# Attention ahead of RWKV, retention behind it, with banks reserved and new costs in a list scheduler

## The chip, the cores and the metric

The kernel runs on one core of one Trainium2 chip. The metric is the device time of one execution in microseconds (us). The kernel before takes 1000.04 us, the median of three executions (999.21 to 1001.67).

Engines go by their short names: PE is TensorE, DVE VectorE, ACT ScalarE, POOL GpSimd, and SP the queue that issues the DMAs.

## The reference, cut to what matters

Two layers over one sequence of 256 tokens, model width 1024. Each layer projects the normed input once, cuts the result into three branches and the gates, and mixes the branches:

```python
def hybrid_layer(x, ...):
    h = _rms(x) * norm1_g
    proj = h @ w_in                       # 1024 -> 768 + 1792 + 2048 + 3072 columns
    aq, ak, av, rw, rq, rk, rv, rg, gates = _split(proj, IN_SIZES)
    ...
    o_a = sliding_window_attention(aq, ak, av, attn_sinks) @ w_attn_o
    o_b = rwkv7_time_mix(rw, ...) @ w_rwkv_o      # a recurrence over tokens, then a group norm
    o_c = retention(rq, rk, rv, rg) @ w_ret_o     # chunks of 128, then a norm and a gate
    g = jax.nn.sigmoid(gates).reshape(B, T, N_BRANCH, D)
    mixed = g[:, :, 0] * o_a + g[:, :, 1] * o_b + g[:, :, 2] * o_c
    x = x + mixed @ w_out
    h2 = _rms(x) * norm2_g
    return x + (jax.nn.silu(h2 @ w_ffn_gate) * (h2 @ w_ffn_up)) @ w_ffn_down   # width 2816
```

The end of RWKV, to which one part of the change belongs, is `y = (y * lnx_g + lnx_b + bonus) * g` with `y` normed by head, `bonus` a row sum times `v`, and `g` a small product of its own.

## The kernel before, in words

**Weights.** All weights are fp32 and are read once, in 292 units of 512 KB. A unit comes by DMA into a tile `raw`, ACT casts it to `wh`, DVE takes `wl = raw - wh` (`wunit`), and PE then runs three products for every tile of output: `wh` with the input's high part, `wl` with the high part, `wh` with the input's low part (`mm3`). There are three tiles each of `raw`, `wh` and `wl`, so the `wl` of a unit can be written only when PE has done with the unit three places ahead of it. These products are called bulk here; each unit holds 12 of them with 512 columns (24 with 256 columns in RWKV's projection `pf`).

**Order.** Nothing is issued as it is written. A recording layer (`class Program`) keeps every operation with its reads and writes, and a list scheduler (`schedule`, `forward`) then puts them into one order per engine: it goes by a cost for each operation (`cost`), latencies between engines (`LAT_*`), and a priority that is mostly the longest path to the end (`bl`). Two things are fixed ahead of it: bulk products stand on PE exactly in the order in which they are recorded, and an engine works its list in order, so a row that waits holds up all rows behind it. PSUM has four banks for bulk results and four (`pss`) for everything small.

**One layer as it is recorded.** Projection `rq` with its rotary embedding; RWKV's projection `pf` in seven blocks; the rest of RWKV (`rwkv_rest`); attention's projections `aq`, `akv` and attention; projections `rk`, `rv`, `rg` and retention; then the gates' projections `gt` and the products `po` with the three output weights, in the order attention, retention, RWKV; `w_out` (`px`); the FFN (`pfg`, `pfu`, `pd`). "Recorded" settles the order of bulk; the small operations of a branch drift to where their inputs and the scheduler's priorities let them.

**What the steps below touch.** In RWKV, X, GA and GR are built from the projections; then DVE inverts 32 by 32 triangles by a chain of 31 pairs `prod`, `Tt` (`Tt` grows by one column a pair), and transposes the result twice into `M` and `Tn`; PE's `pz` reads `Tn`; a recurrence of four steps follows (`pr`, `pu`, `py`, `pd`). The end of RWKV for each half t of the tokens: reduce, POOL's power `ggr`, five products and sums on `ysb` (with `lnx`, `bv` and the product `pgt`), PE transposes `pto`, and a split into `obh` and `obl`, which the last bulk `po` reads. Retention for each half t: `pst`, a mask into `sT`, `po` (PE, from `rv_sb`, `sT` and for t = 1 `Rz`), a square on ACT (`rsq`), a reduce (`rvr`), POOL's power (`rrr`), two products (`o` on DVE, with `rrr` and with `rg_sb`), transposes `ptc`, and a split into `och` and `ocl`, which the bulk `po` of retention reads. Two different things carry the name `po`: bulk ones read `wh` or `wl`, small ones read `sT` or `Rz`.

All operations come from one place in the recording layer, so every row of the profile has the line L421 (L432 in the changed kernel), and rows are told apart by their tiles.

Of the kernel before, what the change touches and what calls it, by code (L numbers as in the profile page):

```python
# [27 lines left out]
LAT_SAME, LAT_X, LAT_IN, LAT_SIDE, LAT_OUT, LAT_DMA, LAT_ISSUE = 130, 150, 250, 400, 200, 930, 1290  # L28
# [79 lines left out]
class Program:  # L108
# [9 lines left out]
    def __init__(self, nc):  # L118
        self.nc, self.ops, self.acc, self.tiles, self.tags, self.bulk = nc, [], {}, {}, {}, False
        self.stream, self.split, self.urgent, self.unit, self.after = 0, False, False, 0, None  # L120
        self.bundle = None
# [35 lines left out]
    def cost(self, eng, method, args, kw, out, ins):  # L157
# [3 lines left out]
        if eng == "PE":  # L161
            if method == "transpose":
                return 109
            if kw["lhsT"].dtype == F32R:
                return 3 + n / 2.4
            c = max(4 + 4 * n / 2.4, 60)
            return c if out.ap[0][1] > 64 else (0.67 if out.ap[0][1] > 32 else 0.36) * c
        src = any(_psum(a) for a in ins)
        if eng == "DVE":
            if method == "reciprocal":  # L170
                return 69 + 6.3 * n
            if method == "tensor_reduce":
                n = 1
                for _, c in list(ins[0].ap)[1:]:
                    n *= c
            if method in ("tensor_copy", "tensor_scalar", "memset") and not src:
                return 69 + n / 1.92
            return 69 + n / 0.96
        if eng == "ACT":
            c = (51 if src else 94) + n / 1.2  # L180
            if _is_ap(kw.get("scale", 1.0)) or _is_ap(kw.get("bias", 0.0)):
                c += 25 if kw["func"] == AF.Copy and not src else 93
# [16 lines left out]
    def add(self, eng, method, fn, args, kw):  # L199
# [15 lines left out]
        touched = []  # L215
# [21 lines left out]
        if merged is not None:  # L237
            assert merged["eng"] == eng
            merged["calls"].append((fn, args, kw))
            merged["touch"].update(touched)  # L240
            merged["cost"] += cost
# [3 lines left out]
        self.ops.append(dict(eng=eng, calls=[(fn, args, kw)], preds=preds, touch=set(touched),  # L245
# [18 lines left out]
    def schedule(self):  # L264
# [15 lines left out]
        for i in range(n - 1, -1, -1):  # L280
            bl[i] = ops[i]["cost"] + max((bl[j] + l for j, l in succ[i]), default=0.0)
        return self.forward(succ, need, bl)

    def forward(self, succ, need, bl):
# [13 lines left out]
        parked = {}  # L298
# [21 lines left out]
        def blocked(i):  # L320
# [6 lines left out]
            for (k, q), ts_ in new.items():  # L327
# [6 lines left out]
                if len(free[k]) < taken[k]:  # L334
                    return k
# [93 lines left out]
def hybrid_kernel(ctx: ExitStack, tc: tile.TileContext, A: dict, cst_d: bass.AP, out: bass.AP, layers=L):  # L429
# [33 lines left out]
    def bc(ap, shape):  # L463
        return ap.to_broadcast(shape)
# [194 lines left out]
    for l in range(layers):  # L659
# [17 lines left out]

        def rope(ps, t):
# [13 lines left out]
        def rope_T(ps, dstT, keep=None):  # L692
            for t in range(2):
                t1, t2 = rope(ps, t)
                if keep is not None and t == 0:
                    qr = keep
                else:
                    qr = ST([128, 512], "qr")
                tt(qr, t1, t2, ADD)
                pt = PS([128, 512], "ptr")  # L700
                transposes(pt, qr)
                S.copy(dstT[:, :, t * 128:(t + 1) * 128], pt.rearrange("p (k t) -> p k t", k=4))

        rec.stream = 2
        ps = proj_tok(2560, 512, "rq")
        rqT = MT([128, 4, T], "rqT")
        rope_T(ps, rqT)
# [88 lines left out]
        def rwkv_rest():  # L796
# [45 lines left out]

            GA = RT([128, 4, 4, 64], "GA")
# [17 lines left out]

            BKT = [RT([128, 2, 4, 128], "BKT") for _ in range(2)]
            for i in range(2):
                for src in (na, EN):
                    pt = PS([128, 2, 2, 128], "ptb")
                    for j in range(2):
                        for d in range(2):
                            P.transpose(pt[:, j, d, :], src[:, 2 * i + j, d * 128:(d + 1) * 128], ident)
                    for par in range(2):
                        o_ = HR[par] if src is na else HR[1 - par]  # L870
                        cs = slice(64 * par, 64 * par + 64)
                        for ci in range(2):
                            S.copy(BKT[i].rearrange("p j (d c) v -> p j d c v", c=2)[o_, :, :, ci, cs], pt[HR[ci], :, :, cs])

# [52 lines left out]
            rk = RT([128, 4, T], "rk")  # L927
            for p in range(4):
                stt(rk[:, p, :], zr[:, p, :], vcol("rk", p), k2[:, p, :], MUL, MUL)
            pbs = head_sums(rk, "pbs")  # L930
            bsum = TL(sm_p, [128, 2, 8], F32, tag="bsum", name="bsum")
            S.copy(bsum.rearrange("p t (a b) -> p t a b", b=2), pbs)


            ysb = [RT([128, 8, 64], "ysb") for _ in range(2)]
            Sn = None
            for c in range(4):
# [4 lines left out]
                for p in range(4):  # L942
                    for par in range(2):
                        mm(pr[HR[par], p, :], X[p][:, par, c, 0:64], sv[:, p, par, :])
# [7 lines left out]
                for p in range(4):  # L952
                    for par in range(2):
                        mm(pu[HR[par], p, :], M[HR[par], p, c, :], RS[HR[par], p, :])
                S.copy(ysb[t][rr], py[rr])
                S.copy(sv[HR[0], :, 0, :], pu[HR[0]])
                S.copy(sv[HR[1], :, 1, :], pu[HR[1]])
                if c < 3:
                    pd = PS([128, 4, 64], "pd")
                    for p in range(4):  # L960
# [26 lines left out]
            rec.after = None  # L987
            ob.extend([None, None])
# [3 lines left out]
            for t in range(2):  # L992
# [13 lines left out]
                bv = ST([128, 8, 64], "bv")  # L1006
                tt(bv, vt[:, t, :].rearrange("p (h v) -> p h v", h=8), bc(bsum[:, t, :].unsqueeze(2), [128, 8, 64]), MUL)
                bvf = bv.rearrange("p h v -> p (h v)")
                tt(bvf, bvf, lnx[:, 1, :], ADD)
# [15 lines left out]
        rec.stream = 3  # L1025
        psq = proj_tok(0, 512, "aq")
        psk = proj_tok(512, 256, "akv")

        qs = [TL(m_p, [128, 2, 4, 128], F32R, tag="m", name="aqs") for _ in range(2)]
        ks = TL(z_p, [128, 2, T], F32R, tag="aks", name="aks", bufs=1)  # L1030
        av, rqs = [], []
        for t in range(2):
            q = ST([128, 512], "q_sb")
            kv = TL(z_p, [128, 256], F32, tag="kv", name="kv")
            act(q, psq[t], AF.Copy, scale=rs[:, t:t + 1])
            act(kv, psk[t], AF.Copy, scale=rs[:, t:t + 1])
            av.append(kv)
            sq = ST([128, 512], "asq")
            ss = TL(sm_p, [128, 10], F32, tag="ass", name="ass")
            act(sq, q, AF.Square)  # L1040
            V.tensor_reduce(out=ss[:, 0:8], in_=sq.rearrange("p (h v) -> p h v", h=8), axis=AX.X, op=ADD)
            sk = ST([128, 128], "ask")
            act(sk, kv[:, 0:128], AF.Square)
            V.tensor_reduce(out=ss[:, 8:10], in_=sk.rearrange("p (h v) -> p h v", h=2), axis=AX.X, op=ADD)

            ts(ss[:, 0:8], ss[:, 0:8], 64e-6, None, ADD)
            ts(ss[:, 8:10], ss[:, 8:10], 1.0 / 64, 1e-6, MUL, ADD)
            rq_ = TL(sm_p, [128, 10], F32, tag="arq", name="arq")
            G.tensor_tensor(out=rq_, in0=ss, in1=C("mh")[:, :10], op=ALU.pow)
            q3 = q.rearrange("p (h v) -> p h v", h=8)  # L1050
            rqs.append(rq_)
            qn = ST([128, 512], "qn")
            qn4 = qn.rearrange("p (g k v) -> p k g v", g=4, k=2)
            for kvh in range(2):
                tt(qn4[:, kvh], q3[:, kvh * 4:kvh * 4 + 4, :], bc(qng[:, l, 0:1, :], [128, 4, 64]), MUL)
            k3 = kv[:, 0:128].rearrange("p (h v) -> p h v", h=2)
            tt(k3, k3, bc(rq_[:, 8:10].unsqueeze(2), [128, 2, 64]), MUL)
            tt(k3, k3, bc(qng[:, l, 1:2, :], [128, 2, 64]), MUL)
            pt = PS([128, 512], "pta")
            transposes(pt, qn)  # L1060
            p4 = pt.rearrange("p (k t) -> p k t", k=4)
            for kvh in range(2):
                r_, q_ = HR[kvh], HR[1 - kvh]
                S.copy(qs[t][r_, kvh], p4[r_])
                tt(qs[t][q_, kvh], p4[r_], qs[t][r_, kvh].bitcast(F32), SUB)
            pt = PS([128, 128], "ptk")
            P.transpose(pt, kv[:, 0:128], ident)
            tk = slice(t * 128, (t + 1) * 128)
            for kvh in range(2):
                r_, q_ = HR[kvh], HR[1 - kvh]  # L1070
                S.copy(ks[r_, kvh, tk], pt[r_])
                S.copy(ks[q_, kvh, tk], pt[r_])
                tt(klz[r_, kvh, tk], pt[r_], ks[r_, kvh, tk].bitcast(F32), SUB)
        oah = TL(o_p, [128, 4, T], F32R, tag="o", name="oah")
        oal = TL(o_p, [128, 4, T], F32R, tag="o", name="oal")
        sink = snk[:, l * 8:l * 8 + 8]
        for t in range(2):
            nk = 128 * (t + 1)
# [244 lines left out]
```

## Time and profile before

| what | value |
|---|---|
| time, median of three | 1000.04 us |
| the profiled execution's own time | 997.55 us |
| its span (first to last instruction) | 995.7 us |
| PE busy | 968.9 us, 97% of the span |
| PE's mean granted clock | 0.995 |
| DVE, ACT, POOL busy | 678.8, 525.7, 40.0 us |
| weights read | 157.01 MB at a mean of 159 GB/s |

The profiled execution lies 2.5 us under the median, and its span 1.85 us under its own time. Busy time of PE is modelled from pipelined products, whose records overlap: a bulk product has a record of 0.39 us, but one starts every 0.23 us. What counts is therefore where PE stands idle, and how far apart equal products start.

### The profile page before, as it was taken

The page shows a single profiled execution, that of the slowest core. Times are in us where ns is not written, and L with a number is a line of the kernel's source. Part 1 is how long each engine was busy: PE and PEld are TensorE (multiplying, and loading weights), DVE is VectorE, ACT ScalarE, POOL GpSimd, SP SyncE. Part 2 cuts the span into 40 slices and gives each one's busy share as a digit, 9 for nine tenths or more (in the row PEclk, how much of TensorE's full clock was granted, in tenths as well). Part 3 has the DMA queues.
Part 4 walks back from the last instruction along what each step waited for, and adds up shares of the span by engine and source line. Part 5 has one row for each costly group of instructions (what it writes and reads, how often), then busy time and mean ns, then how long its engine had stood idle before and what let it go on. Part 6 is the DMA issues. An engine that isn't in the chain of part 4 may idle for free.

```text
span 995.7 us, 15100 instructions
## 1 busy us (share of the span) xinstructions
PE 968.9 (97%) x5894; PEld 801.6 (81%) x5894; DVE 678.8 (68%) x1054; ACT 525.7 (53%) x828; POOL 40.0 (4%) x37
## 2 busy tenths in 40 slices
PE   8999999999899999999999999999996999999998
PEld 7998778878588888898889977688774888888886
DVE  5789968995766555555477998489846675555443
ACT  6756676445347444444366556844552474444432
POOL 1012001000100000000001010010001000000000
PEclk9999999999999999999999999999997999999999
DMA  7645533553346666655654544436621456666562
GB/s 240 183 149 172 163 111 128 165 155 105 112 155 184 178 188 190 188 173 187 190 170 148 165 137 129 143 107 189 191 66 64 151 172 196 184 188 188 175 207 104
DMA packets 93265, 159.04 MB, mean 160 GB/s; under 512 B 5798, under 2 KB 26506, under 8 KB 93194
## 3 DMA queue, kind: packets, MB, share of 16 engines
q1 hardware_dynamic: 93194, 158.08, 52.3%
q8 instruction: 46, 0.75, 0.3%
q14 instruction: 25, 0.20, 0.1%
HBM read 157.01 MB, written 1.05 MB: 159 GB/s over the span
## 4 chain that ended last, share of the span: by engine, by line
PE 84%; DVE 9%; ACT 4%; issue 2%; DMA 1%; POOL 1%; ACTq 0%; DVEq 0%; SPq 0%; POOLq 0%
PE pd L421 13%; PE pfg L421 12%; PE pfu L421 12%; PE gt L421 11%; PE po L421 7%; PE pf L421 6%; PE px L421 4%; DVE wl L421 3%; PE rv L421 2%; PE rg L421 2%; PE rq L421 2%; PE py L421 1%; DVE X L421 1%; ACT sc L421 1%; ACT wh L421 1%
## 5 line engine op out<-in xcount | busy, mean ns | idle before, releaser
L421 DVE TENSOR_TENSOR wl<-raw,wh 128x1024 fp32r<-128x1024 f32 x292 | 356.8, 1223 | 245.7 <-ACT wh L421 244.7
L421 ACT CAST wh<-raw 128x1024 fp32r<-128x1024 f32 x292 | 306.4, 1051 | 322.8 <-PE pd L421 67.5
L421 PE MATMUL gt<-wl,hth 128*128 128x512 f32 x192 | 77.3, 403 | 0.4 <-DVE wl L421 0.4
L421 PE MATMUL gt<-wh,htl 128*128 128x512 f32 x192 | 77.2, 402 | 0.0
L421 PE MATMUL gt<-wh,hth 128*128 128x512 f32 x192 | 76.5, 398 | 0.0
L421 PE MATMUL pfg<-wh,htl 128*128 128x512 f32 (+1 forms) x192 | 72.3, 377 | 0.0
L421 PE MATMUL pfg<-wl,hth 128*128 128x512 f32 (+1 forms) x192 | 72.3, 376 | 0.0
L421 PE MATMUL pfg<-wh,hth 128*128 128x512 f32 (+1 forms) x192 | 71.7, 374 | 0.0
L421 PE MATMUL pfu<-wh,hth 128*128 128x512 f32 (+1 forms) x192 | 71.3, 371 | 0.0
L421 PE MATMUL pfu<-wl,hth 128*128 128x512 f32 (+1 forms) x192 | 71.3, 371 | 0.0
L421 PE MATMUL pfu<-wh,htl 128*128 128x512 f32 (+1 forms) x192 | 71.3, 371 | 0.0
L421 PE MATMUL pd<-wl,ath 128*128 128x512 f32 x176 | 69.8, 396 | 0.0
L421 PE MATMUL pd<-wh,atl 128*128 128x512 f32 x176 | 69.7, 396 | 0.0
L421 PE MATMUL pd<-wh,ath 128*128 128x512 f32 x176 | 69.6, 395 | 0.0
L421 PE MATMUL pf<-hth,wl 128*128 128x256 f32 x224 | 64.0, 286 | 0.0
L421 PE MATMUL pf<-htl,wh 128*128 128x256 f32 x224 | 63.8, 285 | 0.0
L421 PE MATMUL pf<-hth,wh 128*128 128x256 f32 x224 | 63.5, 284 | 0.0
L421 PEld LDWEIGHTS gt<-wl,hth 128*128 128x128 f32 x192 | 36.1, 188 | 9.0 <-DVE wl L421 1.2
L421 PEld LDWEIGHTS pf<-htl,wh 128*128 128x128 f32 x224 | 42.9, 191 | 0.4 <-issue 0.3
L421 PEld LDWEIGHTS pf<-hth,wh 128*128 128x128 f32 x224 | 42.9, 191 | 0.1
L421 PEld LDWEIGHTS pf<-hth,wl 128*128 128x128 f32 x224 | 42.9, 191 | 0.0
L421 PEld LDWEIGHTS gt<-wh,htl 128*128 128x128 f32 x192 | 36.1, 188 | 7.4 <-issue 0.4
(322 smaller groups left out, 1951.9 us busy)
## 6 DMA issues: line engine op xcount, KB each, us to landing
raw<-in_w_in_dram SPq DMA_DIRECT2D x120, 512.0 KB, 3.8
raw<-in_w_ffn_gate_dram SPq DMA_DIRECT2D x44, 512.0 KB, 3.8
raw<-in_w_ffn_up_dram SPq DMA_DIRECT2D x44, 512.0 KB, 3.7
raw<-in_w_ffn_down_dram SPq DMA_DIRECT2D x44, 512.0 KB, 3.6
raw<-in_w_out_dram SPq DMA_DIRECT2D x16, 512.0 KB, 3.6
raw<-in_w_attn_o_dram SPq DMA_DIRECT2D x8, 512.0 KB, 3.6
raw<-in_w_ret_o_dram SPq DMA_DIRECT2D x8, 512.0 KB, 4.2
raw<-in_w_rwkv_o_dram SPq DMA_DIRECT2D x8, 512.0 KB, 3.7
```

The costliest lines, as they stand in the source:

```text
L421: fn(*args, **kw)
```

## The change

- **Order of the branches.** Attention's columns `aq`, `akv` and all of attention are recorded first, ahead of RWKV's projection; retention's are recorded behind RWKV, as `rq`, `rv`, `rg`, `rk`. The bulk order of a layer is so `aq`, `akv`, `pf`, `rq`, `rv`, `rg`, `rk`, `gt`, ... where it was `rq`, `pf`, `aq`, `akv`, `rk`, `rv`, `rg`, `gt`, ...
- **Order inside RWKV.** The transposes BKT and the row sums `bsum` are recorded ahead of GA and GR; the products of `pr`, `pu` and `pd` are each kept together; one of two copies of `pu` goes from ACT to DVE.
- **RWKV's end.** `pgt`, `ag = lnx0 * pgt` and `bg = (bonus + lnx1) * pgt` (both in a tile `ab`) are worked out ahead; behind the recurrence stay one product with `ag`, one with `gr` and one sum with `bg`. The loads of `lnx` wait for the start of the recurrence instead of its end.
- **The scheduler.** New costs and latencies; paths through RWKV's small operations count 2.5 times (CROWD); an operation that needs more than one `pss` bank and finds too few now keeps operations of other branches with a lower priority from taking any.

```diff
-LAT_SAME, LAT_X, LAT_IN, LAT_SIDE, LAT_OUT, LAT_DMA, LAT_ISSUE = 130, 150, 250, 400, 200, 930, 1290
+LAT_SAME, LAT_X, LAT_IN, LAT_SIDE, LAT_OUT, LAT_DMA, LAT_ISSUE = 45, 60, 160, 310, 200, 930, 1290
+CROWD = 2.5
...
             if kw["lhsT"].dtype == F32R:
-                return 3 + n / 2.4
+                return 13.5 + n / 2.4
...
-            return 69 + n / 0.96
+            return (210 if method == "scalar_tensor_tensor" else 150) + n / 0.96
         if eng == "ACT":
-            c = (51 if src else 94) + n / 1.2
+            c = (155 if src else 200) + n / 1.2
...
-            bl[i] = ops[i]["cost"] + max((bl[j] + l for j, l in succ[i]), default=0.0)
+            crowd = CROWD if ops[i]["stream"] == 1 and not ops[i]["bulk"] else 1.0
+            bl[i] = crowd * ops[i]["cost"] + max((bl[j] + l for j, l in succ[i]), default=0.0)
...
                 if len(free[k]) < taken[k]:
+                    if ops[i]["wide"]:
+                        short.add(i)
+                    return k
+                if any(bl[j] > bl[i] and ops[j]["stream"] != ops[i]["stream"] for j in parked.get(k, ()) if j in short):
                     return k
...
+        rec.stream = 3
+        psq = proj_tok(0, 512, "aq")
+        psk = proj_tok(512, 256, "akv")
+        rec.stream = 0
...
-                S.copy(sv[HR[1], :, 1, :], pu[HR[1]])
+                V.tensor_copy(sv[HR[1], :, 1, :], pu[HR[1]])
...
-            rec.after = rec.latest(1)
+            rec.after = begun
...
+            for t in range(2):
+                pgt = PS([128, 512], "pgt")
+                mm(pgt, sg[:, t * 128:(t + 1) * 128], g2)
+                bv = ST([128, 8, 64], "bv")
+                tt(bv, vt[:, t, :].rearrange("p (h v) -> p h v", h=8), bc(bsum[:, t, :].unsqueeze(2), [128, 8, 64]), MUL)
+                bvf = bv.rearrange("p h v -> p (h v)")
+                tt(bvf, bvf, lnx[:, 1, :], ADD)
+                a_ = RT([128, 2, 512], "ab")
+                tt(a_[:, 0], lnx[:, 0, :], pgt, MUL)
+                tt(a_[:, 1], bvf, pgt, MUL)
...
-                tt(yf, yf, lnx[:, 0, :], MUL)
-                tt(yf, yf, bvf, ADD)
-                pgt = PS([128, 512], "pgt")
-                mm(pgt, sg[:, t * 128:(t + 1) * 128], g2)
-                tt(yf, yf, pgt, MUL)
+                tt(yf, yf, bg[t], ADD)
...
         rec.stream = 2
-        ps = proj_tok(3072, 512, "rk")
-        rkT = MT([128, 4, T], "rkT")
-        kr0 = KT([128, 512], "kr0")
-        rope_T(ps, rkT, keep=kr0)
+        ps = proj_tok(2560, 512, "rq")
+        rqT = MT([128, 4, T], "rqT")
+        rope_T(ps, rqT)
         ps = proj_tok(3584, 512, "rv")
...
+        ps = proj_tok(3072, 512, "rk")
+        rkT = MT([128, 4, T], "rkT")
```

How the instructions move is seen best at three places. The first is PE at the end of retention in layer 0, where the half t = 1 leaves its small products (`po<-rv_sb,sT`) and its transposes `ptc` follow. Before:

```order
L421 MATMUL po<-rv_sb,sT 128x64 x2
L421 MATMUL po<-wh,oah 128x512
L421 MATMUL po<-wl,oah 128x512
L421 MATMUL po<-wh,oal 128x512
...
L421 MATMUL po<-wl,oah 128x512
L421 MATMUL ptc<-cst,o_502 128x128 x4
L421 MATMUL po<-wh,oal 128x512
L421 MATMUL gt<-wh,hth 128x512
```

And now, with the bulk that reads `och` and `ocl` right behind:

```order
L432 MATMUL po<-Rz,rqT 128x128
L432 MATMUL po<-rv_sb,sT 128x64 x2
L432 MATMUL po<-wh,ocl 128x512
L432 MATMUL ptc<-cst,o_501 128x128 x4
L432 MATMUL po<-wh,och 128x512
L432 MATMUL po<-wl,och 128x512
...
L432 MATMUL pz<-Tn,GA 32x32 x32
L432 MATMUL po<-wl,och 128x512
L432 MATMUL po<-wh,ocl 128x512
L432 MATMUL gt<-wh,hth 128x512
```

Before, 41 bulk products of attention's output stand between the last `po<-rv_sb,sT` and `ptc`, and 49 more bulk products behind `ptc` ahead of the first that reads `och`; now one stands between, and of the 24 products that read the first columns of `w_ret_o` two stand ahead of the small products, one ahead of `ptc`, 19 between `ptc` and `pz`, and two behind `pz`. Layer 1 has the same rows.

The second place is DVE over the same stretch. Before, at the end of the chain of `prod` and `Tt`:

```order
L421 TENSOR_TENSOR prod<-Y,Tt 128x2x30
L421 TENSOR_TENSOR Tt<-Tt,prod 128x2x30
L421 TENSOR_TENSOR prod<-Y,Tt 128x31
L421 TENSOR_TENSOR wl<-raw,wh 128x1024
L421 TENSOR_TENSOR Tt<-Tt,prod 128x31
L421 STREAM_TRANSPOSE M<-Tt 128x32x2x16
L421 SCALAR_TENSOR_TENSOR tg<-tg,po 128x512
L421 STREAM_TRANSPOSE Tn<-Tt 128x32x2x16
L421 SCALAR_TENSOR_TENSOR tg<-tg,po 128x512
L421 TENSOR_TENSOR wl<-raw,wh 128x1024
```

Now one `wl`, then 25 rows of the chain and ten of retention, then `M` and `Tn`, and only then the next `wl`:

```order
L432 TENSOR_TENSOR wl<-raw,wh 128x1024
L432 TENSOR_TENSOR Tt<-Tt,prod 128x13x19
L432 TENSOR_TENSOR sT<-pst,cst 128x4x128
...
L432 TENSOR_REDUCE rvr<-rsq 128x8
...
L432 TENSOR_TENSOR o_501<-o_501,rg_sb 128x512
...
L432 TENSOR_TENSOR ocl<-ptc,och 128x4x128
L432 STREAM_TRANSPOSE M<-Tt 128x32x2x16
L432 STREAM_TRANSPOSE Tn<-Tt 128x32x2x16
L432 SCALAR_TENSOR_TENSOR tg<-tg,po 128x512
L432 TENSOR_TENSOR wl<-raw,wh 128x1024
```

The ten rows of retention among them are two `sT`, two `ocl` (of t = 0 and t = 1), three `rvr`, one `rrr` and two `o`, with `M` and `Tn` of RWKV behind. The `wl` at the head belongs to the `gt` unit that stands on PE behind `pz`, so it waits for the end of the last `gt` unit ahead of the rows of the first place.

The third place is PE at the end of RWKV, from the last `py` of the recurrence to the transposes `pto`. Before, layer 1 (in layer 0, 25 products `gt` stand between the first `pgt` and the first `pto`):

```order
L421 MATMUL py_1168<-SV,GR 64x64 x4
L421 MATMUL py_1169<-SV,GR 64x64 x4
L421 MATMUL pgt<-g_977,sg 128x512
L421 MATMUL pto<-cst,ysb 128x128
L421 MATMUL pgt<-g_977,sg 128x512
L421 MATMUL pto<-cst,ysb 128x128 x7
L421 MATMUL po<-wh,obh 128x512
```

Now, in both layers (here layer 0):

```order
L432 MATMUL py_380<-SV,GR 64x64 x4
L432 MATMUL pgt<-g_139,sg 128x512 x2
L432 MATMUL po<-wh,ocl 128x512
...
L432 MATMUL gt<-wl,hth 128x512
L432 MATMUL pto<-cst,ysb 128x128 x4
L432 MATMUL gt<-wh,htl 128x512
...
L432 MATMUL gt<-wl,hth 128x512
L432 MATMUL pto<-cst,ysb 128x128 x4
L432 MATMUL gt<-wh,htl 128x512
```

Between the `pgt` and the first `pto` stand now 69 bulk products (10 of retention's output, 59 `gt`), 12 `gt` between the two groups of `pto`, and 25 `gt` ahead of the first product that reads `obh`.

More of the change, by code (lines that the diff above doesn't have):

```diff
@@ L240, in add @@
             merged["touch"].update(touched)
+            merged["wide"] = sum(self.tiles[t][0][0] == "pss" for t in merged["touch"]) > 1
             merged["cost"] += cost
@@ L297, in forward @@
         ready = {e: [] for e in wait}
-        parked = {}
+        parked, short = {}, set()
         tfree = {e: 0.0 for e in wait}
@@ L694, in rope_T @@
                 t1, t2 = rope(ps, t)
[L695 to L698, printed above, removed]
+                qr = keep if keep is not None and t == 0 else t1
                 tt(qr, t1, t2, ADD)
                 pt = PS([128, 512], "ptr")
+                rec.goal = (dstT,)
                 transposes(pt, qr)
+                rec.goal = ()
                 S.copy(dstT[:, :, t * 128:(t + 1) * 128], pt.rearrange("p (k t) -> p k t", k=4))
-        rec.stream = 2
@@ L840, in rwkv_rest @@
                     tt(X[p][r_, par, :, 64:128], c4(zr[r_, p, :]), EI[r_, p, :, 1:65], MUL)
+            BKT = [RT([128, 2, 4, 128], "BKT") for _ in range(2)]
+            for i in range(2):
+                for src in (na, EN):
+                    pt = PS([128, 2, 2, 128], "ptb")
+                    for j in range(2):
+                        for d in range(2):
+                            P.transpose(pt[:, j, d, :], src[:, 2 * i + j, d * 128:(d + 1) * 128], ident)
+                    for par in range(2):
+                        o_ = HR[par] if src is na else HR[1 - par]
+                        cs = slice(64 * par, 64 * par + 64)
+                        for ci in range(2):
+                            S.copy(BKT[i].rearrange("p j (d c) v -> p j d c v", c=2)[o_, :, :, ci, cs], pt[HR[ci], :, :, cs])
+            rk = RT([128, 4, T], "rk")
+            for p in range(4):
+                stt(rk[:, p, :], zr[:, p, :], vcol("rk", p), k2[:, p, :], MUL, MUL)
+            pbs = head_sums(rk, "pbs")
+            bsum = TL(sm_p, [128, 2, 8], F32, tag="bsum", name="bsum")
+            S.copy(bsum.rearrange("p t (a b) -> p t a b", b=2), pbs)
             GA = RT([128, 4, 4, 64], "GA")
@@ L925, in rwkv_rest @@
                 G.memset(SV[0][HR[par], 0, :, par, :], 0.0)
[L927 to L932, printed above, removed]
+            begun = rec.latest(1)
             ysb = [RT([128, 8, 64], "ysb") for _ in range(2)]
@@ L941, in rwkv_rest @@
                 pr = PS([128, 4, 64], "pr")
-                for p in range(4):
-                    for par in range(2):
-                        mm(pr[HR[par], p, :], X[p][:, par, c, 0:64], sv[:, p, par, :])
+                with rec.together():
+                    for p in range(4):
+                        for par in range(2):
+                            mm(pr[HR[par], p, :], X[p][:, par, c, 0:64], sv[:, p, par, :])
                 RS = ST([128, 4, 64], "RS")
@@ L987, in rwkv_rest @@
             rec.after = None
+            ag, bg = [], []
+            for t in range(2):
+                pgt = PS([128, 512], "pgt")
[7 more added lines that the diff above has]
+                tt(a_[:, 1], bvf, pgt, MUL)
+                ag.append(a_[:, 0])
+                bg.append(a_[:, 1])
             ob.extend([None, None])
@@ L1022, in hybrid_kernel @@
         rec.stream = 0
[L1025 to L1073, printed above, removed]
@@ L1148, in hybrid_kernel @@
             rg.append(g_)
+        ps = proj_tok(3072, 512, "rk")
+        rkT = MT([128, 4, T], "rkT")
+        kr0 = KT([128, 512], "kr0")
+        rope_T(ps, rkT, keep=kr0)
         Rz = TL(z_p, [128, 4, 128], F32, tag="Rz", name="Rz", bufs=1)
```

189 lines of the change are left out of this document (110 added, 79 removed).

## The prediction, as it stood before the run

> **What bounds the kernel now.** I read the page's busy shares and its chain of waits first, to see which engine sets the time.
>
> ```profile
> PE 968.9 (97%) x5894; PEld 801.6 (81%) x5894; DVE 678.8 (68%) x1054; ACT 525.7 (53%) x828; POOL 40.0 (4%) x37
> PE 84%; DVE 9%; ACT 4%; issue 2%; DMA 1%; POOL 1%; ACTq 0%; DVEq 0%; SPq 0%; POOLq 0%
> ```
>
> PE is the bound, and both orders hold the same PE instructions. So the change can only move the time in which PE stands idle, or runs at a lower clock. Where that is, the table by stretches shows (the columns are the stretch, its length, busy time of PE, PEld, DVE, ACT and POOL with counts, the granted clock, the share of the DMA engines and GB/s). I cut it at the stages that I knew from the timeline.
>
> ```profile
> 17.00:65.00 48.00, 46.56 (x362) 44.48 (x363) 35.41 (x63) 29.71 (x50) 3.81 (x1) 1.00 0.62 184
> 65.00:120.00 55.00, 54.02 (x348) 45.27 (x347) 53.53 (x99) 34.86 (x67) 5.26 (x2) 1.00 0.52 154
> 120.00:150.00 30.00, 29.19 (x211) 21.35 (x209) 20.79 (x35) 20.37 (x45) 0.00 (x0) 1.00 0.42 124
> 259.00:274.00 15.00, 11.04 (x58) 7.70 (x58) 13.60 (x22) 6.01 (x8) 2.83 (x3) 1.00 0.35 120
> 306.00:437.00 131.00, 131.00 (x650) 110.76 (x649) 74.53 (x87) 68.17 (x89) 0.70 (x1) 1.00 0.63 183
> 500.00:555.00 55.00, 54.33 (x414) 51.70 (x413) 43.47 (x80) 36.75 (x62) 3.68 (x3) 1.00 0.50 148
> 555.00:610.00 55.00, 54.15 (x359) 44.40 (x358) 52.75 (x98) 32.52 (x65) 4.32 (x2) 1.00 0.54 160
> 610.00:700.00 90.00, 89.44 (x497) 70.28 (x496) 69.54 (x123) 52.28 (x89) 4.40 (x3) 1.00 0.48 143
> 754.00:759.00 5.00, 0.89 (x2) 0.06 (x1) 4.97 (x10) 1.23 (x2) 0.00 (x0) 1.00 0.17 42
> 759.00:762.00 3.00, 0.01 (x1) 0.01 (x2) 2.91 (x6) 0.00 (x0) 1.90 (x1) 0.59 0.33 128
> 762.00:770.00 8.00, 7.07 (x19) 4.82 (x20) 4.06 (x6) 1.17 (x2) 0.72 (x1) 0.51 0.00 0
> ```
>
> The FFN (306 to 437) has no idle time at all, and nothing of it changes. The end of RWKV (259 to 274 in layer 0, 754 to 770 in layer 1) has most of it, and layer 1 pays a second time: the clock falls to about a half near 759.5 and is back near 769.8 (0.59 over 3 us and 0.51 over 8 us fix both points). PE's waits by what ended them say what was late there:
>
> ```profile
> PE pto L421 <- DVE ysb L421: 11.3, 4, 7.1
> PE pz L421 <- DVE Tn L421: 1.7, 2, 0.9
> ```
>
> **The change part by part.** *RWKV's end goes under cover: a gain.* What PE loses there now: 15 - 11.04 = 3.96 us in layer 0; 4.11 + 2.99 + 0.93 = 8.03 us in layer 1. The half clock costs more: 7.07 us of work at 0.51 would be 3.6 us at full clock; some of that is the ends of records, so I take 3.2. Together 15.2 us. In the new order the first `pto` has 69 bulk products and two `pgt` ahead of it. What a product costs is shown by a stretch of the chain in which 48 follow each other, 10.91 / 48 = 0.227 us, and what DVE needs for the tail now by the first `pto` of layer 1:
>
> ```profile
> 202.05 10.91 PE gt L421 x48
> 761.99 0.47 PE L421 MATMUL pto<-cst,ysb 128*128 128x128 f32 x1 [7.11 <-DVE ysb L421]
> 268.86 0.33 PE L421 MATMUL pto<-cst,ysb 128*128 128x128 f32 x1 [2.14 <-DVE ysb L421]
> ```
>
> 69 x 0.227 + 2 x 0.43 (half of the 0.89 us in the row from 754) = 16.5 us of cover, against 0.9 + 7.1 = 8.0 us from the first `pgt` to `ysb` in layer 1, and against 25 `gt`, 5.7 us, in layer 0, which fell 2.1 us short. DVE has `wl` rows in between, as in layer 0, and two fewer passes over `ysb`. So the whole 15.2 us goes; bounds 12 (the second half t = 1, with 12 `gt` ahead of it, still waits) and 16.
>
> *`pz`.* Its two waits, about 1 us each, are replaced by the one below: a gain of 2.0 us there (1.7 in the view; idle around it makes the rest).
>
> *Attention's small waits: a gain.* The other stretches above lose 1.44, 0.98, 0.81, 0.67, 0.85 and 0.56 us, 5.3 us together. In 65 to 120 and 555 to 610 DVE is 97% and 96% busy, with attention and RWKV's X at once; attention's work now falls into 17 to 65, where DVE is at 74%. What only RWKV's own chain makes late stays. Bounds 0 and 5.3; I take 4.0, since most rows lie where DVE is full.
>
> *Retention's end: a loss.* This is the part that speaks against the change. The chain of retention, as it ran for t = 1 in layer 0:
>
> ```profile
> 174.75 0.56 PE L421 MATMUL po<-rv_sb,sT 128*128 128x64 f32 x4
> 175.34 0.60 ACT L421 ACTIVATE rsq<-po 128x512 f32<-128x512 f32 x1 [1.91 <-PE po L421]
> 177.57 1.78 POOL L421 TENSOR_TENSOR rrr<-rvr,cst 128x8 f32<-128x8 f32 x1 [2.00 <-DVE rvr L421]
> 183.06 0.69 DVE L421 TENSOR_TENSOR o<-o,rg_sb 128x512 f32<-128x512 f32 x1
> ```
>
> From the last small product to the end of `o` it took 183.75 - 175.31 = 8.4 us, hidden by 41 bulk products. Now one product, 0.23 us, stands there, and behind `ptc` come products that read its result. What DVE has to do in this stretch is fixed by its order, since the `wl` at its head can't come early: it waits until PE has left the last `gt` unit, and then for a cast and itself.
>
> ```profile
> L421 DVE TENSOR_TENSOR wl<-raw,wh 128x1024 fp32r<-128x1024 f32 x292 | 356.8, 1223 | 245.7 <-ACT wh L421 244.7
> L421 ACT CAST wh<-raw 128x1024 fp32r<-128x1024 f32 x292 | 306.4, 1051 | 322.8 <-PE pd L421 67.5
> 196.45 0.42 DVE L421 TENSOR_TENSOR Tt<-Tt,prod 128x247 f32<-128x247 f32 x1
> 215.79 0.18 DVE L421 TENSOR_TENSOR Tt<-Tt,prod 128x31 f32<-128x31 f32 x1
> 216.01 2.04 DVE L421 STREAM_TRANSPOSE M<-Tt 128x1024 f32<-128x1024 f32 x1
> 218.48 2.31 DVE L421 STREAM_TRANSPOSE Tn<-Tt 128x1024 f32<-128x1024 f32 x1
> L421 DVE TENSOR_TENSOR sT<-pst,cst 128x512 f32<-128x512 f32 x8 | 5.5, 690 | 1.1 <-PE pst L421 1.1
> ```
>
> After the last `gt`: 1.05 + 1.22 and two handovers, 2.4 us, to the end of that `wl`. Then 25 rows of the chain (the same sizes ran from 196.45 to 215.79; their durations add up to 8.0 us), seven rows of 512 columns at 0.69 (two `sT`, two `ocl`, two `o`, the `rvr` reduce), 4.8 us, three small ones of about 0.2, and 2.04 + 2.31: 17.8 us. Neighbours that don't depend on each other overlap by 0.1 (`Tn` starts 2.47 after `M`, with a 0.69 us row between them): minus 1.5. Two waits inside the list are not hidden, for `rsq` about 0.7 and for POOL's 1.78 about 0.4: plus 1.1. So `Tn` ends 2.4 + 17.4 = 19.8 us after the last `gt`, and `pz` can start. PE's own work up to `pz`, priced by this run's rows:
>
> ```profile
> 660.56 1.16 PE L421 MATMUL pst<-rqT,rkT 64*128 64x128 f32 x16
> 196.47 5.59 PE po L421 x24
> 173.41 0.56 PE L421 MATMUL po<-rv_sb,sT 128*128 128x64 f32 x4
> 174.08 0.56 PE L421 MATMUL po<-rv_sb,sT 128*128 128x64 f32 x4
> 184.72 0.60 PE L421 MATMUL ptc<-cst,o 128*128 128x128 f32 x4
> ```
>
> `pst` 1.1; four groups of small `po` at 0.67 (174.08 - 173.41) 2.7; eight `ptc` 1.0; 22 bulk products at 5.59 / 24 = 0.233, 5.1; switches 0.2: 10.1 us. PE stands idle for 19.8 - 10.1 = 9.7 us, about 5.8 of it in one piece ahead of `ptc`. The second path, from `ocl` of t = 1 through 17 bulk products (4.0 us) to `pz`, ends at the same time, so neither alone would shorten it. Both layers have these rows: 19.4 us; bounds 8.5 and 11 a layer, by the handovers.
>
> *The clock in this stall.* No such idle stretch of 5.8 us is in the trace. The nearest rows: 7.1 us in layer 1 brought the half clock, 4.7 us after PE fell idle (754.9 to 759.5), for 10.3 us; 2.1 us in layer 0 did not (1.00 in the row from 259). [...] Between 0 and 2.6, I take 1.5 a layer, 3.0 in all, as 5.8 is nearer to 7.1. [...]
>
> *The rest.* The other small rows keep their number; BKT, `bsum` and the copy on DVE lie beside bulk with `wl` 1 us or more ahead (if DVE's slack there were gone, each would cost its own 0.4 us). The loads of `lnx` move past nothing that waits. The start is alike: eight units of `aq` instead of `rq`. All of this is 0, between -1 and 2.
>
> Sum against the profiled execution: -15.2 - 2.0 - 4.0 + 19.4 + 3.0 = +1.2 us, 998.8 for its 997.55. The median lies 2.5 us higher: 1001.
>
> **The rivals.** What a measurement of this kernel can tell from no change is about 0.3%, 3 us.
>
> *The forecast*, within that: gain and loss cancel, 1001; its own range 997 to 1003. Chance 0.40.
>
> *Slower: the stall takes the clock with it in both layers, in full.* The place is the idle stretch ahead of `ptc`; it decides when that passes the 4.7 us after which the clock fell in 754 to 759. Price: 2.6 instead of 1.5 a layer, and the bulk of the slowed stretch feeds `wl` later, which takes back half of attention's 4.0: +1.2 + 2.2 + 2.0 = +5.4, 1005.5. For it speaks that 5.8 is over 4.7; against it that small products and `och` break up the idle time. Chance 0.26.
>
> *Slower: RWKV's end isn't emptied.* The products with `ab` and `ggr` stand behind eight `wl` rows on DVE; if those hold `ysb` beyond the 16.5 us of cover in layer 1, some 8 us don't come back: 1009. The 8 us of tail in 754 to 762 had one `wl`. Chance 0.05.
>
> *Faster: the stall is idle time alone.* The clock stays at 1.00, as in layer 0's tail, attention's 5.3 us go in full, and the list on DVE runs at its lower end: 2 x 8.5 to 9.7 - 15.2 - 2.0 - 5.3 = -5.5 to -3.1, 994.5 to 997. For it: no single idle piece here is as long as 7.1. Against it: DVE's list has no slack. Chance 0.29.
>
> **How the numbers follow.** The likeliest is 1001. To leave out no more than 2 in 10, the range takes the faster case's lower end and the main slower case with its bounds: 994 to 1007. Faster 0.29, within 0.3% 0.40, slower 0.26 + 0.05 = 0.31.
>
> **What would show it.** In the changed profile: no wait of `pto` for `ysb` over 0.5 us, and the clock at 1.00 through both ends of RWKV; PE idle for some 10 us a layer between the last `gt` ahead of retention's products and `pz`, ended by `o` ahead of `ptc` and by `Tn` ahead of `pz`; DVE full over the same time; the clock there at 0.5 or not. Wrong would be: an idle time there under 5 us a layer (then faster), `pto` still waiting (slower), or new waits of bulk for `wl` in the first 60 us of a layer.

## The result, and the profile after

The changed kernel takes 992.17 us (990.79 to 992.94), the kernel before 1000.86: a ratio of 0.9914, interval 0.9895 to 0.9932. That is 8.7 us less where about 1 us more was forecast, and 1.8 us under the range. The profiled executions lie 6.8 us apart (997.55 and 990.79); the runs of before spread over some 4 us (the last section comes back to that).

The granted clock before, in 40 slices of the span, and then the busy times and the granted clock of the changed kernel:

```profile
PEclk9999999999999999999999999999997999999999
PE 964.6 (98%) x5894; PEld 800.7 (81%) x5894; DVE 686.7 (69%) x1066; ACT 522.8 (53%) x820; POOL 45.9 (5%) x37
PEclk9999999989999999999999999997999999999999
```

Before, the clock was lower in one place, RWKV's end in layer 1. Now it is lower in two, both at the stall ahead of `ptc`. The waits of PE, by what ended them (total, times, longest):

```profile
PE ptc L432 <- DVE o L432: 11.8, 4, 5.7
...
PE po L432 <- DVE sT L432: 1.4, 4, 0.5
PE po L432 <- ACT och L432: 1.4, 2, 0.7
```

`pto` and `pz` are gone from this list, `ptc` stands at its head, as forecast. The stretch itself, layer 0 on PE and DVE (start, length):

```profile
191.03 0.30 PE L432 MATMUL ptc<-cst,o 128*128 128x128 f32 x1 [0.32 <-DVE o L432]
...
197.59 0.56 PE L432 MATMUL po<-rv_sb,sT 128*128 128x64 f32 x4
...
204.15 1.09 PE L432 MATMUL ptc<-cst,o 128*128 128x128 f32 x4 [5.71 <-DVE o L432]
...
210.74 1.20 PE L432 MATMUL pz<-Tn,GA 32*32 32x32 f32 x64
...
198.87 0.69 DVE L432 TENSOR_REDUCE rvr<-rsq 128x8 f32<-128x512 f32 x1 [0.31 <-ACT rsq L432]
...
203.31 0.69 DVE L432 TENSOR_TENSOR o<-o,rg_sb 128x512 f32<-128x512 f32 x1
203.91 0.27 DVE L432 TENSOR_TENSOR prod<-Y,Tt 128x112 f32<-128x112 f32 x1
...
206.54 1.95 DVE L432 STREAM_TRANSPOSE M<-Tt 128x1024 f32<-128x1024 f32 x1
208.34 2.25 DVE L432 STREAM_TRANSPOSE Tn<-Tt 128x1024 f32<-128x1024 f32 x1
```

PE left the last `gt` at 191.03 - 0.32 = 190.71 and reached `pz` at 210.74, 20.0 us later, when `Tn` had just ended (208.34 + 2.25 = 210.59). The same stretches by the table (length, busy PE, ..., clock), and RWKV's recurrence and end behind them:

```profile
191.00:204.20 13.20, 6.10 (x48) 4.78 (x49) 12.53 (x31) 2.55 (x4) 2.25 (x2) 0.87 0.42 131
204.20:208.00 3.80, 3.80 (x12) 3.16 (x13) 3.57 (x9) 0.59 (x1) 0.61 (x2) 0.55 0.02 4
677.00:692.40 15.40, 8.30 (x48) 6.79 (x48) 12.76 (x32) 2.80 (x4) 1.73 (x1) 0.66 0.37 121
692.40:696.00 3.60, 3.60 (x11) 3.01 (x12) 3.36 (x10) 0.59 (x1) 0.61 (x2) 0.54 0.00 0
734.20:773.30 39.10, 39.10 (x177) 31.40 (x176) 31.89 (x44) 18.16 (x22) 5.98 (x2) 1.00 0.51 162
```

RWKV's end (734 to 773 in layer 1) is now full and at full clock; the 13 to 15 us ahead of `ptc` have PE at half load with DVE at 95% and 83%.

Busy time alone does not add up to the difference. So I took every pair of neighbouring products on PE and counted how much further apart their starts lie than the median of that shape. This is what "by starts" means below. The medians add up to the same 934.3 us in all kernels, since all hold the same products; the rest is lost time, here of both layers, in us, with three kernels of the next section beside. Grouping the products by tile as well as by shape moves a level by up to 5 us, a difference between two kernels by under 2 us, and one between before and after by 1 us at most:

| stage | before | after | before_order | after_oldcosts | before_costs |
|---|---|---|---|---|---|
| projections | 16.1 | 9.0 | 16.7 | 13.6 | 11.7 |
| gates to `pz` (retention's end) | 5.5 | 26.9 | 2.6 | 1.6 | 24.9 |
| recurrence | 5.4 | 1.9 | 5.7 | 0.9 | 12.7 |
| RWKV's end | 17.4 | 1.1 | 1.0 | 1.9 | 10.0 |
| start, `w_out`, FFN | 9.2 | 7.8 | 7.9 | 8.1 | 7.9 |
| sum | 53.6 | 46.7 | 33.8 | 26.1 | 67.2 |

### The profile page after: what moved, and what is told of

Its sections match the earlier page's. It is cut to its first block, busy times and chain, and to the rows that moved or that the text cites. A ratio compares the mean times of both kernels' runs of the same rounds, so it can differ in the third digit from the quotient of the medians.

```text
span 988.8 us, 15098 instructions
## 1 busy us (share of the span) xinstructions
PE 964.6 (98%) x5894; PEld 800.7 (81%) x5894; DVE 686.7 (69%) x1066; ACT 522.8 (53%) x820; POOL 45.9 (5%) x37
## 4 chain that ended last, share of the span: by engine, by line
PE 91%; DVE 2%; issue 2%; DMA 2%; POOL 1%; ACT 1%; SPq 0%; ACTq 0%; DVEq 0%; POOLq 0%
PE pd L432 13%; PE gt L432 12%; PE pfg L432 12%; PE pfu L432 12%; PE po L432 8%; PE pf L432 7%; PE px L432 4%; PE rk L432 2%; PE rg L432 2%; PE rv L432 2%; PE rq L432 2%; PE py L432 2%; DMA raw<-in_w_in_dram 1%; PE aq L432 1%; PE poa L432 1%
## 5 line engine op out<-in xcount | busy, mean ns | idle before, releaser
L432 PEld LDWEIGHTS gt<-wh,hth 128*128 128x128 f32 x192 | 36.1, 188 | 8.0 <-issue 1.1
```

The costliest lines, as they stand in the source:

```text
L432: fn(*args, **kw)
```

## The experiments

All are timed beside the kernel before, which had medians of 998.2 to 1001.4 us there.

**The stall covered (gc_ahead).**

```diff
-        for cb in range(2):
-            gc = gates(2, cb)
-            mix_part(2, wr_o, (och, ocl), cb, gc)
+        gcs = [gates(2, 0), gates(2, 1, KT)]
+        for cb in range(2):
+            mix_part(2, wr_o, (och, ocl), cb, gcs[cb])
```

> The changed kernel with both blocks of retention's gate projection (96 products gt) recorded ahead of retention's output products, instead of 48 and then 24 products, twice. On PE 28 bulk products (6.4 us) now stand between retention's last small product and ptc, and 50 between ptc and pz. Theory (the idle time ahead of ptc is the price of where retention stands in the bulk order): PE idle at ptc falls from 5.7 us to under 1 us in each layer, pz waits under 1 us, RWKV's end keeps only 29 gt and two pgt (7.5 us) as cover and waits 1 to 4 us a layer; 974 to 982 us. Rival (DVE has too much to do in this stretch wherever retention stands): the 10 to 12 us of a layer come back ahead of pz or pto; 988 us or more.

989.01 us, ratio 0.9893 (0.9870 to 0.9917): the rival. The wait ahead of `ptc` fell from 5.7 to 1.2 us. But with more bulk ahead of it PE reached `pz` at 707.4 in layer 1 instead of 698.9, and RWKV's end had only its 29 `gt` left:

```profile
PE pto L432 <- DVE ysb L432: 5.9, 4, 2.3
PE ptc L432 <- DVE o L432: 2.5, 2, 1.2
```

By starts, some 15 us less are lost ahead of `pz` in both layers, and some 13 us more at RWKV's end. What the bulk covers in one place it uncovers in the other; the medians of the two kernels are 3 us apart, and their intervals overlap. DVE's order is another one here as well: four `wl` stand among the rows of the chain in this stretch, and two between `M` and `Tn`.

**RWKV's end alone (before_tail)**: the kernel before with this part of the change, nothing else.

```diff
-            rec.after = rec.latest(1)
+            rec.after = begun
...
+                tt(a_[:, 0], lnx[:, 0, :], pgt, MUL)
+                tt(a_[:, 1], bvf, pgt, MUL)
...
+                tt(yf, yf, ag[t], MUL)
                 tt(y, y, bc(gr, [128, 8, 64]), MUL)
-                tt(yf, yf, lnx[:, 0, :], MUL)
-                tt(yf, yf, bvf, ADD)
...
-                tt(yf, yf, pgt, MUL)
+                tt(yf, yf, bg[t], ADD)
```

> The kernel before with RWKV's end alone changed (pgt, ag and bg worked out ahead; lnx loaded from the start of the recurrence). On PE 40 gt then stand between the last py and pto, and 20 between its two halves, in place of 25 and 0. Theory (RWKV's end is the largest gain and the rest of the change costs): the waits of pto go and with them the half clock, 15 to 17 us less than before; 983 to 987 us. Rival (the gain is in attention's place and in the costs; RWKV's end alone only moves its wait to another place): 994 us or more, with a wait ahead of pz or ptc in place of that at pto.

990.32 us, 0.9907 (0.9883 to 0.9931): between the two. Layer 0's end is emptied (lost time 5.4 to 0.4 us); in layer 1, whose order has no bulk there, 9.5 of 12.0 stay:

```profile
PE pto L421 <- DVE ysb L421: 5.5, 1, 5.5
```

**The former end in the changed kernel (after_oldtail)**: the diff above the other way round.

> The changed kernel with RWKV's end as it was before. On PE one pgt and 84 bulk products stand between the last py and the first pto, then 6 gt between the halves. Theory (what empties RWKV's end is the bulk that the new order leaves behind the recurrence, not the shorter chain): the first pto doesn't wait, the second waits 0 to 2 us a layer; 992 to 996 us. Rival (the shorter chain is needed): pto waits 4 us or more a layer; 1000 us or more.

990.33 us, 0.9897 (0.9867 to 0.9927): the theory, and more. `pto` is not among its waits. The shorter end gains nothing that can be seen where bulk stands behind the recurrence.

**The former costs (after_oldcosts)**: constants and the body of `cost` as before, and

```diff
-CROWD = 2.5
+CROWD = 1.0
```

> The changed kernel with the scheduler's former costs and latencies and without CROWD; branch order, reservation and RWKV's end stay. On PE 37 bulk products stand between retention's last small product and ptc, and 69 behind it ahead of the first that reads och; RWKV's end has 66 bulk products ahead of the first pto, one between the halves. Theory (the weight on RWKV's paths is what pushed retention to the end and made the stall): no wait at ptc, up to 2 us at pz and 3 us at the second pto in each layer, attention's stretch as in the changed kernel; 975 to 984 us. Rival (the new costs are where the gain is): waits of bulk for wl and of small products return in attention's stretch; 993 us or more.

970.56 us, 0.9707 (0.9685 to 0.9730): the theory's side, 4 us under its range. Nothing but the scheduler's numbers differs from the changed kernel, and the stall is gone. That the weight made it, as the theory says, this run can't tell, since it sets back the costs and latencies as well. In the profiled execution PE is never idle for long and its clock stays full:

```profile
PE pz L430 <- DVE Tn L430: 1.0, 2, 0.5
PE pto L430 <- DVE ysb L430: 0.7, 2, 0.4
...
143.40:204.30 60.90, 60.10 (x325) 49.23 (x324) 56.09 (x105) 27.62 (x33) 4.69 (x5) 1.00 0.54 158
PEclk9999999999999999999999999999999999999999
```

**Which of the new numbers (after_nocrowd, oldcosts_crowd, oldcosts_newlat, after_oldlat, after_crowd_both).** The first two set CROWD alone, to 1 in the changed kernel and to 2.5 with the former costs:

> The changed kernel with CROWD = 1 (no weight on RWKV's paths), its other costs kept. On PE 47 bulk products stand ahead of retention's second ptc, 57 more gt ahead of pz than the products that read och, and none between the last py and pto. Theory (weight and costs only choose which of two chains on DVE is late: retention's, hidden by gates, or RWKV's, whose end is bare without the weight): no wait at ptc, but pto waits 6 us or more in each layer, with the clock at a half; 986 to 998 us. Rival (the weight makes the stall and nothing else needs it): 968 to 978 us.

1001.45 us, 1.0019 (1.0001 to 1.0036): the theory's mechanism, 3 us over its range. `ptc` doesn't wait; RWKV is late instead, and its recurrence waits too, which I had not counted:

```profile
PE pto L432 <- DVE ysb L432: 11.5, 2, 5.8
PE pd L432 <- ACT SV L432: 2.8, 4, 1.6
PE pr L432 <- DVE SV L432: 1.6, 2, 1.4
```

> The changed kernel with the former costs and latencies but with CROWD = 2.5. On PE 36 bulk products stand ahead of retention's second ptc and 67 behind it ahead of the first that reads och; 51 bulk products stand ahead of the first pto and 20 between the halves. Theory (the stall comes with the new costs, not with the weight): no wait over 1 us at ptc and pto; 966 to 973 us. Rival (the weight makes the stall): 985 us or more.

971.62 us, 0.9721 (0.9695 to 0.9747): the theory; the weight alone does no harm. The next two exchange the latencies alone. The first is after_oldcosts with the new ones; the second is the changed kernel with the former ones:

```diff
-LAT_SAME, LAT_X, LAT_IN, LAT_SIDE, LAT_OUT, LAT_DMA, LAT_ISSUE = 45, 60, 160, 310, 200, 930, 1290
+LAT_SAME, LAT_X, LAT_IN, LAT_SIDE, LAT_OUT, LAT_DMA, LAT_ISSUE = 130, 150, 250, 400, 200, 930, 1290
```

> The changed kernel with the former durations and no CROWD, but with the new latencies. On PE 30 bulk products stand ahead of retention's second ptc in layer 0, 30 in layer 1, and 44 and 51 gt ahead of the first pto. Theory (the new durations make the stall, the latencies don't): no wait over 1 us at ptc or pto; 966 to 974 us. Rival (the latencies do): 985 us or more.

976.57 us, 0.9786 (0.9760 to 0.9811): between, nearer to the theory; `pz` waits 3.1 us in all, `ptc` 0.8. So the new latencies alone cost 6 to 8 us against after_oldcosts, by medians and by ratios.

> The changed kernel with the former latencies, but its new durations and CROWD. On PE retention's second ptc stands behind pz and ptv with no bulk product in between. Theory (the new durations with the weight on RWKV alone make the stall): PE idle 5 us or more a layer between retention's last small product and the bulk that reads och; 985 to 999 us. Rival (the latencies do): 975 us or less.

985.52 us, 0.9865 (0.9838 to 0.9892): just the theory; `ptc` waits twice 2.5 us, and by starts some 9 us a layer are lost between the gates and `pz`. So the large loss comes with the new durations: at the new branch order, all kernels of this section that have them take 984 us or more, and all without them 978 or less. The latencies add their 6 to 8 us without them, and 5 to 7 with them (992.2 against 985.5). The weight costs about 1 us with the former numbers, but beside the new ones it saves 9 to 10 (992.2 against 1001.4). The new durations by themselves, with neither the new latencies nor the weight, were not run, nor were PE's, DVE's and ACT's durations exchanged one by one. The last kernel gives retention the weight too:

```diff
-            crowd = CROWD if ops[i]["stream"] == 1 and not ops[i]["bulk"] else 1.0
+            crowd = CROWD if ops[i]["stream"] in (1, 2) and not ops[i]["bulk"] else 1.0
```

> The changed kernel with its new costs, and the weight of 2.5 on retention's paths as well as on RWKV's. On PE five bulk products stand ahead of retention's second ptc and 22 between it and pz. Theory (the stall is retention's lower rank against RWKV on DVE): the wait at ptc falls from 5.7 to 1 to 4 us a layer and pz waits 1 us or less; 972 to 985 us. Rival (DVE is full there whatever the ranks, and what retention gains RWKV loses): 989 us or more.

984.81 us, 0.9864 (0.9838 to 0.9890): faster by 5 to 7 us, and in time just within the theory, but `ptc` still waits 4.7 us a layer. Rank is a part of it, not the whole.

**The branch order alone (before_order)**: whole blocks moved in the kernel before.

```diff
-        rec.stream = 2
-        ps = proj_tok(2560, 512, "rq")
+        rec.stream = 3
+        psq = proj_tok(0, 512, "aq")
+        psk = proj_tok(512, 256, "akv")
...
         rec.stream = 2
-        ps = proj_tok(3072, 512, "rk")
+        ps = proj_tok(2560, 512, "rq")
...
+        ps = proj_tok(3072, 512, "rk")
         Rz = TL(z_p, [128, 4, 128], F32, tag="Rz", name="Rz", bufs=1)
```

> The kernel before with nothing but the branch order changed: attention's projections and attention ahead of RWKV's, retention's behind (rq, rv, rg, rk); costs, scheduler and RWKV as they were. On PE 42 bulk products stand ahead of retention's second ptc, 49 to 64 bulk products ahead of the first pto, 26 and 7 between the halves (before: 25 and 0 ahead, 0 between). Theory (the branch order is the whole gain): 971 to 978 us. Rival (the order inside RWKV, its products kept together, and its end are needed with it): 983 us or more.

977.63 us, 0.9778 (0.9757 to 0.9798): the theory, at its upper end. The table above shows the whole of it at RWKV's end (17.4 to 1.0 us) and at `pz`; the projections gain nothing (16.1 and 16.7).

**The new costs alone (before_costs)**: the new constants and body of `cost` in the kernel before, and

```diff
+            crowd = CROWD if ops[i]["stream"] == 1 and not ops[i]["bulk"] else 1.0
-            bl[i] = ops[i]["cost"] + max((bl[j] + l for j, l in succ[i]), default=0.0)
+            bl[i] = crowd * ops[i]["cost"] + max((bl[j] + l for j, l in succ[i]), default=0.0)
```

> The kernel before with nothing but the new costs, latencies and CROWD. On PE no bulk product stands ahead of the first pto in layer 0, 72 in layer 1; in layer 1 the second ptc of retention stands right behind pz. Theory (the new costs lose by themselves, since they order small work by chains that then stand bare): 1000 to 1012 us. Rival (they gain at the former branch order): 995 us or less.

1011.44 us, 1.0118 (1.0096 to 1.0139): the theory. Its waits stand where its order left chains bare:

```profile
PE pz L425 <- DVE Tn L425: 7.1, 1, 7.1
PE pto L425 <- DVE ysb L425: 6.6, 2, 6.3
PE ptp L425 <- ACT BKT L425: 5.8, 2, 5.4
```

**Products kept together (before_together, oldcosts_apart).** Put into the kernel before, for `pr`, `pu` and `pd`, with the copy of `pu` on DVE; in the second kernel `if True:` stands in place of the three `with` of after_oldcosts:

```diff
-                S.copy(sv[HR[1], :, 1, :], pu[HR[1]])
+                V.tensor_copy(sv[HR[1], :, 1, :], pu[HR[1]])
...
+                with rec.together():
+                    for p in range(4):
+                        for par in range(2):
+                            mm(pr[HR[par], p, :], X[p][:, par, c, 0:64], sv[:, p, par, :])
```

> The kernel before with the products of pr, pu and pd each kept together in the recurrence, and one copy of pu on DVE; nothing else. Theory (the recurrence loses 2.4 to 2.8 us a layer to changes between bulk and small products and half of it goes with fewer changes; the rest of the order is the former one): 996 to 999 us. Rival (the changes cost nothing that the median shows): 1000 us or more.

995.48 us, 0.9960 (0.9945 to 0.9976): the theory, half a us better. With the same 59 bulk products between `pz` and `pgt` in layer 1, that stretch took 751.55 - 714.87 = 36.7 us instead of 753.76 - 716.02 = 37.7, though waits of 1.9 us are in it; it changes between bulk and small products 22 times instead of 32. The copy of `pu` that moved to DVE is in these numbers too.

> The changed kernel with the former costs, no CROWD, and the products of pr, pu and pd free to be parted by bulk again (after_oldcosts, 970.6 us, has them kept together). Theory (fewer changes between bulk and small products in the recurrence are worth about 1.3 us a layer): 972.5 to 974.5 us. Rival (worth nothing): 969.5 to 971.5 us.

972.62 us against 970.56, ratios to before 0.9729 (0.9709 to 0.9749) and 0.9707: the theory's size, though the intervals overlap. The traces bear it out: by starts the recurrence loses 2.9 us more in both layers together, with 68 changes between bulk and small products instead of 52, that is 0.18 us each.

**Reservation and end without the new costs (oldcosts_noreserve, oldcosts_oldtail)**: after_oldcosts with the edit below, and after_oldcosts with RWKV's former end.

```diff
-                    if ops[i]["wide"]:
+                    if False:
```

> The changed kernel with the former costs, no CROWD, and without the reservation of banks. On PE the stretch from retention to pto has the same covers within ten products. Theory (the reservation is worth little where no chain is bare): 968 to 975 us. Rival (it is what keeps attention's and RWKV's small products apart): 980 us or more.

970.14 us, 0.9702 (0.9682 to 0.9722): the theory. The reservation is worth nothing that can be told here; beside the new costs it was not tried.

> The changed kernel with the former costs, no CROWD, and RWKV's end as it was before, so that the branch order, the reservation and the order inside RWKV are what is left of the change. On PE one pgt and 62 bulk products stand ahead of the first pto, 5 gt between the halves. Theory (the branch order is what leaves bulk behind the recurrence, so that RWKV's end is covered in its old form too): pto waits 0 to 2 us a layer; 970 to 976 us. Rival (the shorter end is worth its 15 us here as well): 980 us or more.

972.69 us, 0.9723 (0.9703 to 0.9744): the theory; the end is worth 2 us at most, and the intervals overlap.

**What adds up.** From 1000 us: branch order -22 (before_order, 977.6); order inside RWKV, products together and what else is left -5 (oldcosts_oldtail, 972.7); RWKV's end -2, within the intervals (after_oldcosts, 970.6); new durations, latencies and CROWD +22 (the changed kernel, 992.2). These are differences of medians; the ratios move each by up to 2 us. oldcosts_noreserve and after_oldcosts beat both kernels by 21 us and more.

## Why the prediction was wrong

**Right: the stall.** Forecast were 19.8 us from the last `gt` to `pz` and 1.5 for the clock; measured 20.0 and, in layer 1, 677.27 - 0.32 to 698.91, 22.0. The row of 5.8 us ahead of `ptc` was 5.7. What held `pz` was what the forecast said, DVE's list up to `Tn`. The split was off: PE was idle for 7.4 us of the 20.0 in layer 0, not 9.7, and 3.5 us of its products ran at half clock (0.50, from 204.15 to near 207.6). The clock's price came almost all in layer 1, and that its size is near is partly luck. The forecast chose 1.5 a layer between 0 and 2.6; no run shows the 2.6, an estimate of mine that the slower rival and the range use too. The runs showed half clock for 6.9 us in layer 0 and 13.8 in layer 1. In layer 0 the bulk behind `ptc` ran slowed and `pz` still started with `Tn`, so it cost next to nothing. In layer 1 the small products ran slowed, so DVE waited 2.3 us for `rsq` (up to 687.10) instead of 0.3, and the whole list ended 2 us later. The table has +21.4 us for gates to `pz`; the forecast was 19.4 + 3.0 - 2.0 = +20.4. after_oldcosts, where the same stage loses 1.6 us, shows that this is the price of the new numbers and no part of the branch order.

**Right: RWKV's end.** -16.3 us against -15.2.

**Wrong: "Attention's small waits", 4.0 with a bound of 5.3.** The projections gained 7.1 us. The bound was the step that failed: I read idle time from busy times, and a PE whose records overlap is full in that table while its products start late. By starts, 16.1 us were lost there and not 5.3. The reason was wrong too: attention's earlier place gains nothing in this stage (before_order, 16.7); the new costs do (before_costs, 11.7). They are not all of it: after_oldcosts, without them, loses 13.6.

**Wrong: "The rest ... is 0".** Under it lay the products kept together. The recurrence gained 3.5 us, and before_together shows 3.8 us of time for this edit, with the moved copy, alone. The stretch looked full in before,

```profile
221.00:259.80 38.80, 38.80 (x520) 30.45 (x520) 20.74 (x37) 20.07 (x39) 2.25 (x3) 1.00 0.33 103
```

and it was the same mistake: a change between bulk and small products costs time between starts (0.18 us each in oldcosts_apart; in before_together ten fewer made 37.7 us into 36.7), which no idle time shows.

**Sum.** -1.1 (end), -3.1 (projections), -3.5 (recurrence), -1.4 (start, FFN) and +1.0 (stall) take the forecast +1.2 to -6.9, which is the distance of the two profiled executions. The 1.4 us of start and FFN were put at nothing too; what gave them was not traced. The 2 us more between the medians lie within the spread of before's runs, and the last section shows that its profiled execution was one of its quick ones. The faster rival (994.5 to 997) named the right side and the wrong cause: the clock did fall.

What stays open: how the new durations lead the scheduler to leave retention so late. At the new branch order all slow kernels have them, but how the ranks meet in DVE's queue was not traced. One thing the traces do show: the new durations are not simply truer. The scheduler lets an engine go on to its next row only when the cost of the last one is over, so the cost should be the distance between starts. A DVE row of 512 columns has a record of 0.69 us, but the row behind `o` above starts 203.91 - 203.31 = 0.60 us after it. The former cost gives 69 + 512 / 0.96 = 602 ns, the new one 150 + 512 / 0.96 = 683 ns, the length of the record. (For a row that needs the one ahead of it, cost and latency together come to about the same: 602 + 130 and 683 + 45.) So the new costs make DVE fuller for the scheduler than it is. For bulk on PE the new cost is the better one: 13.5 + 512 / 2.4 = 227 ns, where one starts every 0.227 us and the former cost was 216. For `M` it is the nearer one, 2.2 us against 1.1, where `Tn` starts 208.34 - 206.54 = 1.8 us after it. Whether the rows booked too long are what delays retention was not tested.

## What to carry to other kernels

On an engine that is 97% busy, measure lost time by the distance between starts, shape by shape, before bounding a gain by its idle time. A list scheduler's costs should be held against the same distance and not against the length of a record alone; that this would mend the order here was not tested. When one change holds a reordering and a new cost model, time them apart: here they were worth -22 and +22 us, and their sum looked like a small gain. A wait that is fixed by the order of a second engine (one `wl`, 37 rows, the next `wl`) could be priced to a few tenths here (19.8 us against 20.0 in layer 0), and moving the first engine's work in front of it can uncover a wait elsewhere (gc_ahead: 1.2 us left ahead of `ptc`, but up to 2.3 us ahead of `pto`).

## What the runs showed of the hardware

Where the clock had fallen in these two profiles, it stood at 0.50 of full speed (760.0 to 769.5 in before, 201.0 to 207.5 and 682.5 to 695.5 in the changed kernel). The half clock lasted 10.3 us in before (prediction), and from the rows above 13.2 x 0.13 / 0.5 + 3.8 x 0.45 / 0.5 = 6.9 us in layer 0 of the changed kernel, 15.4 x 0.34 / 0.5 + 3.6 x 0.46 / 0.5 = 13.8 us in layer 1. Unexpected was when it fell. In layer 1 that was near 692.4 - 15.4 x 0.34 / 0.5 = 682, ahead of the long idle stretch: the groups of small products start 0.67 us apart in layer 0 and 1.28 in layer 1,

```profile
195.97 0.44 PE L432 MATMUL po<-Rz,rqT 128*128 128x128 f32 x2
196.64 0.44 PE L432 MATMUL po<-Rz,rqT 128*128 128x128 f32 x2
680.08 0.50 PE L432 MATMUL po<-wh,och 128*128 128x512 f32 x1 [0.68 <-ACT och L432]
681.03 0.43 PE L432 MATMUL po<-rv_sb,sT 128*128 128x64 f32 x2 [0.21 <-DVE sT L432]
681.95 0.59 PE L432 MATMUL po<-rv_sb,sT 128*128 128x64 f32 x2 [0.48 <-DVE sT L432]
682.33 0.74 PE L432 MATMUL po<-Rz,rqT 128*128 128x128 f32 x2
683.61 0.74 PE L432 MATMUL po<-Rz,rqT 128*128 128x128 f32 x2
```

and in the 4.7 us ahead of it PE had been idle for only 0.68 + 0.21 + 0.48 us, with no idle time over 0.7 us in one piece. In layer 0 the same rows with the same waits did not bring the clock down there (1.00 up to 200.5); it fell near 204.2 - 13.2 x 0.13 / 0.5 = 200.8, when PE had been idle for 2.4 us (since 197.95 + 0.48 = 198.43). So in both layers the clock fell sooner than after the 4.7 us of idle time that came ahead of its fall in before. What brings it down these traces do not show.

Where the clock falls thus differs between two like stretches of one execution, and whether the place differs between executions too was not traced. Times differ: 995 to 1003 us for before over all comparisons, 998 to 1004 for after_nocrowd, 970.1 to 971.0 for after_oldcosts, whose clock averaged 0.998 or more in every run. The clock of every execution is on record, and the two go together. Of the 37 executions of before that were timed beside the experiments, the 12 with a mean clock of 0.988 or less took 999.6 to 1002.9 us, the 21 with 0.991 or more 995.1 to 999.9. The profiled execution of before had 0.995, more than all of these but one, and took 2.5 us less than the median. Which of the two sets the other no run tested.
